# Hybrid RWKV-7 and short-convolution block on one NeuronCore: the usual instruction order, with forms, operand requests, norm and gating as deferred steps

## The chip, the cores and the metric

The kernel runs on one core of one Trainium2 chip. The metric is device time in microseconds; the kernel before took 1043.12 us, the median of three runs (1041.12 to 1046.09). Engines are named as in the profile: PE (TensorE), DVE (VectorE), ACT (ScalarE), POOL (GpSimd), SP (SyncE, which here only issues transfers).

## The reference, cut to what matters

All of it is fp32, with one layer, 512 frames plus 16 meta frames, a model width of 2048 and 8320 projected columns.

```python
hn = _rmsnorm(h_res, norm_in_g[l])
P = hn @ w_in[l]                       # [528, 2048] @ [2048, 8320]
...                                    # r, k, v, g_r, low-rank w and a, token shift
y = _rwkv7_recurrence(rh, decay, kh, vh, kk, kk * ah)    # state per head, frame by frame
yn = (y - mean) * rsqrt(var + LNX_EPS)  # per head
y_a = (yn * lnx_g + lnx_b + bonus) * silu(g_r)
y_b = Bg * causal_conv3(Cg * hc) * silu(g_c)
h_res = h_res + concat([y_a, y_b]) @ w_out[l]
out = _rmsnorm(h_res, norm_f_g)[:, 16:]
```

## The kernel before, in words

**Products.** A product in fp32 is made of three in fp32r: every operand is split into a rounded part and the rest ("low"), and high by high, high by low and low by high are summed in PSUM. Raw weights arrive 512 KB at a time (`request`, L216, on SP's queue). For each quarter of 128x512 `split_w` (L221) makes the high part with an ACT cast (L224) and the low part with a subtraction (L225) on DVE or POOL, as `engines` and the table `ON_POOL` say (L51, L228). The operand tiles for it are six ("hl"). The numbers behind a name in the programs' rows tell buffers of one name apart.

**In-projection.** Its columns go tile by tile. Most are single tiles (L440). The last twelve tiles, of the convolution branch, go as six pairs (`PAIRS`, `pair`, L475): seven products of half matrices (M1, P5, Q6, M3, M7, M2, P4), each of two quarters with twelve matmuls, in place of eight. Their weights are sums of raw tiles (L252, on POOL or DVE), their left operands "forms", sums of x that are brought back from memory and split (`form`, `third_form`, L544/L545). Pair results are added up on DVE as products end (L523, L526, L533), scaled by the norm's factor (`scaled`, L630), and convolved and gated (L667, L668, L716 to L720, L731, L739). After the last pair's M7 `restore` (L612) writes a part of x back (L620, L621).

**Recurrence.** Frames go in chunks of 64. Each chunk's inverse matrices are made ahead for two pairs of heads at a time (`invert`, L1159; on PE L1183, L1197, L1199; copies to SBUF on ACT, L1190). Then `recur` (L1280) runs nine chunks while the pairs' products go on. A chunk's steps on PE are L1297 (needs the state `st`), L1314, and L1352/L1356 (`zs`, `zy`); between them ACT copies results (`pn`, L1305, L1319, L1320) and DVE makes the next state (L1365, L1366). A chunk's operands are `ca` and `cb`, loaded from memory (L1263, on SP). `norm` (L1373) follows at once: sums and centring on DVE (L1382, L1383), squares on ACT (L1388), a reduction on DVE (L1389), the power -0.5 on POOL (L1390, L136), scaling and a transpose on DVE (L1394, L1395), four stores on SP (L1399).

**Order.** PE's order is written by hand: chunk steps and matmuls of pairs are interleaved by `fill` with fixed nanoseconds (`FW`), so each chunk step stands between given products. The orders of ACT, DVE, POOL and SP come from the framework's scheduler, here with `schedule_with_timeline_sim=True` (L1883); every engine takes its instructions strictly in that order. `advance` (L242) prepares weights to eight quarters ahead of the one in use, and requests raw tiles for up to three more where their buffer's last reader has been issued (`free`). `later(ns, fn)` runs a step when PE's written order has come that many nanoseconds further; `ahead()` raises a step's priority.

**Output.** `split_mix` splits the mixed branches, and the out-projection runs in two halves of seven products for four column groups (L1598), its weights loaded and split like the others (L1567), followed by the final norm.

## Time and profile before

| what | value |
|---|---|
| median of 3 runs (lowest, highest) | 1043.12 us (1041.12, 1046.09) |
| the profiled execution's own time | 1044.57 us |
| its span | 1042.8 us |
| its mean granted PE clock | 0.982 |
| busy: PE, DVE, ACT, POOL | 995.9, 758.1, 440.3, 377.4 us |

The span covers the instructions of the profiled execution; its own time has 1.77 us more around it. PE's busy share in the profile's forty slices is 9 tenths nearly everywhere but around the middle of the second half. Four stretches matter below: the single tiles with the preparation of the recurrence (25 to 599 us), the last inversion (599 to 625 us), the six pairs with the recurrence (625 to 850 us), and the start of the out-projection (850 to 925 us).

### The profile page before, as it was taken

Reading aid. Unit: us, or ns where it says so; the run is one execution under the profiler, and the core shown is the slowest. Engines: PE = TensorE matmul, PEld = TensorE weight load, DVE = VectorE, ACT = ScalarE, POOL = GpSimd, SP = SyncE. Lnnn points to the kernel's source line nnn. Section 1 sums busy time; section 2 is a strip of 40 time slices with the busy share of each in tenths; the row PEclk is TensorE's granted clock in tenths of the full one; section 3 lists DMA queues with packets and bytes.
Section 4 is the critical chain, followed back from the end, with each engine's and each line's share of the span. In section 5 each row is a group of like instructions: output and inputs, shape, how many; then the busy total and the mean of one; then the engine's idle time right before and its main releaser. Section 6 shows DMA issues by size and latency. Waiting matters only on the chain. (4 is left out here: it accounts for less than half of the span.)

```text
span 1042.8 us, 24382 instructions
## 1 busy us (share of the span) xinstructions
PE 995.9 (96%) x9867; PEld 927.9 (89%) x9867; DVE 758.1 (73%) x1323; ACT 440.3 (42%) x823; POOL 377.4 (36%) x384
## 2 busy tenths in 40 slices
PE   9999998999999999999999979989879898999996
...
GB/s 312 162 107 154 153 202 170 138 155 150 197 177 156 142 179 132 209 153 143 126 135 169 168 223 278 187 230 174 223 180 99 231 297 230 182 268 193 165 121 162
DMA packets 223216, 188.60 MB, mean 181 GB/s; under 512 B 158720, under 2 KB 187136, under 8 KB 222592
## 3 DMA queue, kind: packets, MB, share of 16 engines
...
q14 instruction: 35, 0.29, 0.1%
...
## 5 line engine op out<-in xcount | busy, mean ns | idle before, releaser
L224 ACT CAST w<-wr 128x512 fp32r<-128x512 f32 x288 | 175.1, 618 | 277.8 <-PE ps_k L440 45.4
L225 POOL TENSOR_TENSOR w<-wr,w 128x512 fp32r<-128x512 f32 x151 | 219.5, 1465 | 181.2 <-ACT w L224 151.2
L225 DVE TENSOR_TENSOR w<-wr,w 128x512 fp32r<-128x512 f32 x137 | 102.8, 753 | 46.6 <-ACT w L224 46.3
L440 PE MATMUL ps_k<-xh,w 128*128 128x272 f32 (+1 forms) x512 | 97.7, 288 | 0.0
L440 PE MATMUL ps_v<-xh,w 128*128 128x256 f32 (+1 forms) x512 | 95.2, 284 | 0.0
L440 PE MATMUL ps_r<-xh,w 128*128 128x258 f32 (+1 forms) x512 | 94.4, 281 | 0.0
L440 PE MATMUL ps_g<-xh,w 128*128 128x256 f32 (+1 forms) x512 | 92.2, 281 | 0.0
L440 PEld LDWEIGHTS ps_k<-xh,w 128*128 128x128 f32 x512 | 82.1, 193 | 0.4
L440 PEld LDWEIGHTS ps_v<-xh,w 128*128 128x128 f32 x512 | 79.9, 188 | 0.3
L440 PEld LDWEIGHTS ps_r<-xh,w 128*128 128x128 f32 x512 | 79.7, 188 | 0.1
L440 PEld LDWEIGHTS ps_g<-xh,w 128*128 128x128 f32 x512 | 78.9, 188 | 0.5 <-DVE gt L1007 0.2
L440 PE MATMUL ps_k<-xl,w 128*128 128x272 f32 (+1 forms) x256 | 73.9, 289 | 0.0
L440 PE MATMUL ps_v<-xl,w 128*128 128x272 f32 (+1 forms) x256 | 72.4, 283 | 0.0
L440 PE MATMUL ps_g<-xl,w 128*128 128x258 f32 (+1 forms) x256 | 72.1, 282 | 0.0
L440 PE MATMUL ps_r<-xl,w 128*128 128x258 f32 (+1 forms) x256 | 72.0, 281 | 0.0
L1553 POOL DMA_DIRECT2D x<-in_w_out_dram x16 | 14.3, 891 | 124.9 <-DVE o L1567 122.0
L440 PE MATMUL ps_h<-xh,w 128*128 128x258 f32 (+1 forms) x320 | 58.7, 283 | 0.0
L440 PE MATMUL ps_C<-xh,w 128*128 128x258 f32 (+1 forms) x320 | 57.7, 281 | 0.0
L252 POOL TENSOR_TENSOR wr<-wr,wr 128x512 f32<-128x512 f32 x24 | 35.2, 1473 | 61.2 <-DVE w L225 27.6
L440 PE MATMUL ps_B<-xh,w 128*128 128x512 f32 x160 | 52.6, 394 | 0.0
L440 PE MATMUL ps_gc<-xh,w 128*128 128x512 f32 x160 | 50.5, 392 | 0.0
L440 PEld LDWEIGHTS ps_h<-xh,w 128*128 128x128 f32 x320 | 50.0, 190 | 0.2
...
## 6 DMA issues: line engine op xcount, KB each, us to landing
...
```

What stands on the lines that cost most here:

```text
L224: state["cast"] = nc.scalar.copy(hi, rq).ins
L225: low[n] = eng.tensor_tensor(out=lo, in0=rq, in1=hi.bitcast(F32), op=ALU.subtract).ins
L252: sum_eng.tensor_tensor(out=x, in0=x, in1=held[extra][:, o : o + 512], op=ALU.add)
L440: nc.tensor.matmul(ps[r], ww[:, w], xx[:, kt, a:b], start=(kt == 0 and n == 0), stop=(kt == KT - 1 and n == 2))
L1553: nc.gpsimd.dma_start(chain[g], rows_of(half, k, col, g), accum_op=ALU.add)
```

## The change

The framework's scheduler is called without its timeline simulation, so ACT, DVE, POOL and SP get the order that it gives by default, by priority and by the order in which the code issues steps. PE's rows are the same ones in the same order. With it:

- `advance` prepares operands six quarters ahead of the one in use instead of eight (`LEAD`), requests raw tiles for five more, and adds raw tiles up to two quarters before their split.
- `ON_POOL`: the lows of M7 and one of the two of P4 go from POOL to DVE; in the first pair those of M3 too. That is eight on POOL per pair before, five after, and three in the first pair.
- Forms: loads and splits are spaced by new numbers (`form`, `split`, `seven`, `six`); four of the eight form lows go to POOL, and so do the lows of the third part, which is now loaded in two pieces.
- `norm`'s squares, reduction with power, scaling with transpose, and stores are four steps at 2500, 4500, 9000 and 10500 ns instead of one step with stores at 7000.
- The gate of the last single tile of the convolution branch waits until after the first pair's P5 copy.
- `ca` and `cb` (apart from the first) are issued on ACT's queue instead of SP's, and at other places of the chunk.
- In the output stage the first group's raw tile is loaded once more (512 KB), lows of the first eight mixed tiles go to POOL, and the explicit waits of `behind_low` are gone.

```diff
@@ -43,14 +43,15 @@
-    tr=3200, lev=3000, cp=4200, out=1500, begin=19500, p=2700, u=2700, s=4700, last=3700, mix=2600, form=1000, split=6000, early=60000, apart=48000,
+    tr=3200, lev=3000, cp=4200, out=1500, begin=19500, p=2700, u=2700, s=4700, last=3700, mix=2600, form=200, split=1500, seven=6000, six=9000, early=60000, apart=48000,
 )
-AHEAD, WEIGHTS, FORMS = 6000, 3000, 2000
+AHEAD, WEIGHTS, LEAD = 6000, 3000, 6
+NORM = (2500, 4500, 9000, 10500)
 ON_POOL = {
-    "M1": ((), ()), "P5": ((), ()), "Q6": ((), ()), "M3": ((0, 1), ()), "M7": ((0, 1), (0, 1)), "M2": ((0, 1), ()),
-    "P4": ((0, 1), (0, 1)),
+    "M1": ((), ()), "P5": ((), ()), "Q6": ((), ()), "M3": ((0, 1), ()), "M7": ((), (0, 1)), "M2": ((0, 1), ()),
+    "P4": ((1,), (0, 1)),
 }
@@ -214,7 +216,10 @@
     def request(n):
-        held[n] = chain[n - N_IN] if n >= N_IN else raw_tile(place_of[n], f"wr{n}")
+        if n == N_IN:
+            order.append(order.pop(0))
+            place_of[n] = order[-1]
+        held[n] = chain[n - N_IN] if n > N_IN else raw_tile(place_of[n], f"wr{n}")
         state["dma"] = nc.sync.dma_start(held[n], raws[n]).ins
@@ -230,7 +235,7 @@
             return nc.gpsimd if (n % 2 or late) and 22 < n < S_IN else nc.vector, None
-        low_on, sum_on = ON_POOL[kind[2][0]]
+        low_on, sum_on = ON_POOL["P5" if kind[2][0] == "M3" and n < FIRST_PAIR + 14 else kind[2][0]]
         return (nc.gpsimd if kind[2][1] in low_on else nc.vector), (nc.gpsimd if kind[2][1] in sum_on else nc.vector)
@@ -239,19 +244,28 @@
-    def advance(upto, more=0):
+    def add_up(n):
+        kind, r, o, extra = slots[n]
+        if extra is not None and n not in summed:
+            summed.add(n)
+            x = held[r][:, o : o + 512]
+            engines(n)[1].tensor_tensor(out=x, in0=x, in1=held[extra][:, o : o + 512], op=ALU.add)
+
+    summed = set()
+
+    def advance(upto, more=0, ahead=0):
         end = len(slots) if chain else S_IN
...
             kind, r, o, extra = slots[n]
-            low_eng, sum_eng = engines(n)
             with tc.high_priority(offset=WEIGHTS):
-                x = held[r][:, o : o + 512]
-                if extra is not None:
-                    sum_eng.tensor_tensor(out=x, in0=x, in1=held[extra][:, o : o + 512], op=ALU.add)
-                split_w(n, x, low_eng)
+                add_up(n)
+                split_w(n, held[r][:, o : o + 512], engines(n)[0])
             state["slot"] = n + 1
+            for m in range(n + 1, min(n + 1 + ahead, end)):
+                if slots[m][3] is not None and last_raw(m) < state["raw"]:
+                    add_up(m)
         for n in range(state["slot"], min(upto + more, end)):
@@ -503,19 +521,22 @@
                 state["used"] += 1
-                advance(state["used"] + 8, 3)
+                advance(state["used"] + LEAD, 9 - LEAD + 2, 2)
...
             with ahead():
-                nc.scalar.copy(t[:, 0:n], ps[:, 0:n])
+                state["sum"] = nc.scalar.copy(t[:, 0:n], ps[:, 0:n]).ins
...
         copy(v, B, n_t)
+        if "mixed" in state:
+            with tc.issue_after(state["sum"]):
+                state.pop("mixed")()
         yield from product("Q6", A, n_t)
@@ -574,40 +594,49 @@
         dims, fp = [P, 3, W2], shared_pools[1]
-        t = fp.tile(dims, F32, tag=f"f{KA // 2 + k}", name=f"sum{k}") if k < KA // 2 else temporary(k, f"sum{k}", dims)
-        f = fp.tile([P, 2, 3, LF], F32R, tag=f"f{k}", name=f"forms{k}")[:, :, :, 8 : 8 + W2]
+        if k < 3:
+            t = fp.tile(dims, F32, tag=f"f{4 + k}", name=f"sum{k}")
+        elif k == 3:
+            rest.append(fp.tile([P, 2] + dims[1:], F32, tag="f7", name="sum3"))
+            t = rest[0][:, 0]
+        elif k == 6:
+            t = rest[0][:, 1]
+        else:
+            t = temporary(0 if k == 4 else 1, f"sum{k}", dims)
         nc.sync.dma_start(t, fsum[:, k, 0:3])
         def part():
-            with tc.issue_after(state["ts"]) if k >= 4 else nullcontext():
-                apart(f[:, 0], f[:, 1], t, nc.vector)
-
-        later(FW["split"], part)
-        sfr.append(f)
-
-    thirds = []
+            f = fp.tile([P, 2, 3, LF], F32R, tag=f"f{k}", name=f"forms{k}")[:, :, :, 8 : 8 + W2]
+            sfr[k] = f
+            with tc.issue_after(state["tm"]) if k > 5 else nullcontext():
+                apart(f[:, 0], f[:, 1], t, nc.vector if k in (0, 1, 3, 5) else nc.gpsimd)
+
+        later(FW["split"] if k < 6 else FW["six"] + 500 * k, part)
+
+    rest, thirds = [], {}
     def load_third(j):
-        a, b = 3 * j, min(3 * j + 3, KA)
-        t = temporary(min(j, 1), f"third{j}", [P, 3, W2])[:, 0 : b - a]
+        a, b = ((0, 3), (3, KA))[j]
+        t = (
+            cqt([P, 5 * W2], F32, tag="g", name="third1").rearrange("p (k w) -> p k w", k=5)
+            if j else temporary(0, "third0", [P, 3, W2])
+        )
         nc.sync.dma_start(t, fsum[:, a:b, 3])
-        thirds.append((slice(a, b), t))
+        thirds[j] = (slice(a, b), t)
...
         shared_pools.append(shared.enter_context(tc.tile_pool(name="fp", bufs=1, reuse_waits="tile")))
-        for k in range(KA):
+        for k in range(7):
             later(FW["form"] * k, lambda k=k: form(k))
+        later(FW["form"] * 7, lambda: load_third(1))
+        later(FW["seven"], lambda: form(7))
+        later(FW["seven"] + 500, lambda: load_third(0))
+
+    def third_form():
         for j in range(2):
-            later(FW["form"] * KA, lambda j=j: load_third(j))
-
-    def third_form():
-        assert len(thirds) == 2
-        for j in range(3):
             k, t = thirds[j]
-            apart(xh[:, k, T0X:XW], xl[:, k, T0X:XW], t, nc.vector)
-            if j == 1:
-                load_third(2)
+            apart(xh[:, k, T0X:XW], xl[:, k, T0X:XW], t, nc.gpsimd)
@@ -734,11 +764,18 @@
                 scaled(REAL, ps, g, META)
-            gate(g, f"c{i}")
-            o = direct.get(8 + i, cv)
-            nc.vector.scalar_tensor_tensor(out=o, in0=cv, scalar=0.5, in1=g, op0=ALU.mult, op1=ALU.mult)
-            if o is cv:
-                later(9000, lambda: nc.sync.dma_start(mixd[8 + i], cv))
+
+            def mixed():
+                gate(g, f"c{i}")
+                o = direct.get(8 + i, cv)
+                nc.vector.scalar_tensor_tensor(out=o, in0=cv, scalar=0.5, in1=g, op0=ALU.mult, op1=ALU.mult)
+                if o is cv:
+                    later(9000, lambda: nc.sync.dma_start(mixd[8 + i], cv))
+
+            if i == 3:
+                state["mixed"] = mixed
+            else:
+                mixed()
         ready.add((what, i))
@@ -1258,9 +1295,9 @@
-    def load_ops(t, c, pairs, part):
+    def load_ops(t, c, pairs, part, queue=nc.scalar):
         a, b = pairs
-        nc.sync.dma_start(
+        queue.dma_start(
             t[:, a:b],
@@ -1304,6 +1343,9 @@
             if c and not last:
+                if c == 1:
+                    second[2] = new_second(ch, 2)
+                    load_ops(second[2], 2, (0, 4), 1)
                 load_ops(second[c + 1], c + 1, (4, 8), 1)
@@ -1312,12 +1354,12 @@
                         nc.tensor.matmul(z[e][hs, 1, k], t[m, O_X : O_X + CH], pn[m, e, k], start=True, stop=True)
-            if not last:
-                first[c + 1] = load_first(ch, c + 1)
             u = pn
...
                 nc.scalar.copy(u[:, 1], z[1][:, 1])
+            if not last:
+                first[c + 1] = load_first(ch, c + 1)
             fill(FW["u"])
@@ -1354,9 +1396,6 @@
                         nc.tensor.matmul(d[ho, j], t[hs, o : o + CH], x[hs], start=(a == 0), stop=(a == b - 1))
-            if c + 2 < NCH:
-                second[c + 2] = new_second(ch, c + 2)
-                load_ops(second[c + 2], c + 2, (0, 4), 1)
             if not last:
@@ -1378,21 +1417,33 @@
-        for z, j in zip(zs, (slice(0, NPAIR - 1), slice(NPAIR - 1, NPAIR))):
+        for z, j in zip(zs[::-1], (slice(NPAIR - 1, NPAIR), slice(0, NPAIR - 1))):
             nc.vector.tensor_reduce(out=nv[:, 0, j], in_=z, op=ALU.add, axis=AX.X)
...
         yq = yt.rearrange("p (j s) -> p j s", s=CH)
-        with tc.issue_after(state["cast"]):
+
+        def scale():
+            nc.vector.tensor_reduce(out=nv[:, 1], in_=yq, op=ALU.add, axis=AX.X)
+            nc.gpsimd.tensor_scalar(
+                out=nv[:, 2], in0=nv[:, 1], scalar1=1.0 / CH, scalar2=LNX_EPS, op0=ALU.mult, op1=ALU.add
+            )
+            rsqrt(nv[:, 3], nv[:, 2])
+
+        def turn():
+            nc.vector.tensor_tensor(out=yc, in0=yc, in1=spread(3), op=ALU.mult)
+            nc.vector.transpose(yt, yc.rearrange("p j s -> p (j s)"))
+
+        def square():
             nc.scalar.activation(yq, yc, AF.Square)
-        nc.vector.tensor_reduce(out=nv[:, 1], in_=yq, op=ALU.add, axis=AX.X)
-        nc.gpsimd.tensor_scalar(
-            out=nv[:, 2], in0=nv[:, 1], scalar1=1.0 / CH, scalar2=LNX_EPS, op0=ALU.mult, op1=ALU.add
-        )
-        rsqrt(nv[:, 3], nv[:, 2])
-        nc.vector.tensor_tensor(out=yc, in0=yc, in1=spread(3), op=ALU.mult)
-        nc.vector.transpose(yt, yc.rearrange("p j s -> p (j s)"))
+            if c + 2 < NCH:
+                second[c + 2] = new_second(ch, c + 2)
+                load_ops(second[c + 2], c + 2, (0, 4), 1)
+
+        later(NORM[0], square)
+        later(NORM[1], scale)
+        later(NORM[2], turn)
@@ -1405,7 +1456,7 @@
-        later(7000, put)
+        later(NORM[3], put)
@@ -1677,6 +1726,8 @@
             if half == 0:
+                if g == 0:
+                    at(-1, begin_chain, 0, g)
                 if g == 3:
@@ -1880,7 +1927,7 @@
     args.append(nc.dram_tensor("out_0_dram", (SEQ, DM), F32, kind="ExternalOutput").ap())
-    with tile.TileContext(nc, schedule_with_timeline_sim=True) as tc:
+    with tile.TileContext(nc) as tc:
         hymba_kernel(tc, *args)
```

Three places show how the rows move. The first is DVE at the end of the fifth pair's products, around the state of the sixth chunk (`st_10363` before, `st_10346` after); `yc` and `yt` are the norm's tiles, `gc` and `cv` the gate and the convolution's result, `w` an operand tile, `wr` raw weights. Before:

```order
L630 TENSOR_TENSOR gc_10191<-sums_B_gc_9653,rs 128x256
L252 TENSOR_TENSOR wr_9817<-wr_9817,wr_9947 128x512
L225 TENSOR_TENSOR w_10101<-wr_9817,w_10101 128x512
L1394 TENSOR_TENSOR yc_10062<-yc_10062,nv_10061 128x512
L1395 STREAM_TRANSPOSE yt_10063<-yc_10062 128x512
L630 TENSOR_TENSOR gc_10191<-ps_B_gc_A,rs 128x256
L225 TENSOR_TENSOR w_10117<-wr_9817,w_10117 128x512
L668 SCALAR_TENSOR_TENSOR gc_10191<-th_c_10194,gc_10191 128x512
L739 SCALAR_TENSOR_TENSOR cv_9646<-cv_9646,gc_10191 128x512
L1365 TENSOR_TENSOR st_10363<-zs_10279,st_10058 128x512
```

After:

```order
L1428 TENSOR_REDUCE nv_10044<-yt_10046 128x8
L659 TENSOR_TENSOR gc_10178<-ps_B_gc_A,rs 128x256
L230 TENSOR_TENSOR w_10173<-wr_9801,w_10173 128x512
L1435 TENSOR_TENSOR yc_10045<-yc_10045,nv_10044 128x512
L697 SCALAR_TENSOR_TENSOR gc_10178<-th_c_10181,gc_10178 128x512
L1436 STREAM_TRANSPOSE yt_10046<-yc_10045 128x512
L771 SCALAR_TENSOR_TENSOR cv_9629<-cv_9629,gc_10178 128x512
L230 TENSOR_TENSOR w_10255<-wr_9877,w_10255 128x512
L1404 TENSOR_TENSOR st_10346<-zs_10264,st_10041 128x512
```

The gate's second part from PSUM (L630 before, L659 after) stood behind the norm's scaling and transpose, and now stands ahead of both; the gate's products stay ahead of the state.

The second is DVE in the last pair (`xl` is the part of x that `restore` writes back). Before:

```order
L523 TENSOR_TENSOR sums_B_gc_10734<-ps_B_gc_B,sums_B_gc_10734 128x256
L630 TENSOR_TENSOR b_11048<-sums_B_gc_10734,rs 128x256
L1394 TENSOR_TENSOR yc_10922<-yc_10922,nv_10921 128x512
L621 SCALAR_TENSOR_TENSOR xl<-again_11024,pvt,xh 128x258 x2
L1395 STREAM_TRANSPOSE yt_10923<-yc_10922 128x512
L621 SCALAR_TENSOR_TENSOR xl<-again_11030,pvt,xh 128x258
L526 TENSOR_TENSOR sums_B_gc_10734<-sums_B_gc_10734,ps_B_gc_A 128x256
L621 SCALAR_TENSOR_TENSOR xl<-again_11030,pvt,xh 128x258
L621 SCALAR_TENSOR_TENSOR xl<-again_11036,pvt,xh 128x258 x2
```

After:

```order
L544 TENSOR_TENSOR sums_B_gc_10718<-ps_B_gc_B,sums_B_gc_10718 128x256
L659 TENSOR_TENSOR b_11034<-sums_B_gc_10718,rs 128x256
L1428 TENSOR_REDUCE nv_10906<-yt_10908 128x8
L547 TENSOR_TENSOR sums_B_gc_10718<-sums_B_gc_10718,ps_B_gc_A 128x256
L659 TENSOR_TENSOR b_11034<-sums_B_gc_10718,rs 128x256
L650 SCALAR_TENSOR_TENSOR xl<-again_11010,pvt,xh 128x258 x2
L1435 TENSOR_TENSOR yc_10907<-yc_10907,nv_10906 128x512
L1436 STREAM_TRANSPOSE yt_10908<-yc_10907 128x512
L554 TENSOR_TENSOR sums_B_gc_10718<-ps_B_gc_C,sums_B_gc_10718 128x256
```

The sum that empties M7's PSUM bank, into which PE's P4 goes (L526, now L547), has moved ahead of the norm's scaling and of all rows that write x back.

The third is ACT in the last inversion (`ts` is the copy that PE's L1197 reads). Before:

```order
L224 CAST w_7766<-wr_7761 128x512
L544 CAST forms_7854<-sum_7853 128x3x258
L544 CAST forms_7866<-sum_7865 128x3x258
L224 CAST w_7803<-wr_7801 128x512
L544 CAST forms_7878<-sum_7877 128x3x258
L544 CAST forms_7890<-sum_7889 128x3x258
L1190 COPY ts_0_7927<-t_0_7893 128x512
L1190 COPY ts_1_7928<-t_1_7894 128x512
```

After:

```order
L229 CAST w_7763<-wr_7761 128x512
L229 CAST w_7766<-wr_7761 128x512
L1227 COPY ts_0_7948<-t_0_7914 128x512
L1227 COPY ts_1_7949<-t_1_7915 128x512
L229 CAST w_7803<-wr_7801 128x512
L229 CAST w_7806<-wr_7801 128x512
L564 CAST forms_7882<-sum_7853 128x3x258
```

The two copies (L1190, now L1227) stood behind four casts of forms, and now stand ahead of all of them.

56 lines of the change are left out of this document (28 added, 28 removed).

## The prediction

> **What bounds the kernel now.** I read the table by stretch first, then PE's timeline for its stops, then the chain of waits and the other engines' timelines at those stops. Columns of the first: stretch, length, busy us (instructions) of PE, weight loads, DVE, ACT and POOL, granted PE clock, DMA share, GB/s.
>
> ```profile
> 25.00:599.00 574.00, 568.73 (x5288) 548.64 (x5286) 386.13 (x771) 223.97 (x409) 201.19 (x233) 0.99 0.63 158
> 599.00:625.00 26.00, 20.06 (x289) 16.18 (x283) 19.85 (x30) 13.50 (x22) 4.32 (x3) 0.93 0.69 219
> 625.00:850.00 225.00, 206.22 (x3394) 197.47 (x3383) 169.01 (x235) 88.34 (x182) 144.44 (x105) 0.95 0.70 208
> 850.00:925.00 75.00, 68.79 (x293) 55.43 (x292) 68.37 (x90) 35.24 (x59) 12.99 (x11) 0.98 0.78 215
> ```
>
> PE is the bound: in the single tiles it idles 574 - 568.73 = 5.3 us. In the pairs it idles 225 - 206.22 = 18.8 us, and four stops make up most of that; two more stand in the last inversion. In brackets is the idle time and what ended it.
>
> ```profile
> 601.67 1.13 PE L1183 MATMUL t<-xn,gt 64*64 64x64 f32 x32 [2.46 <-DVE xn L1174]
> 609.43 0.33 PE L1197 MATMUL z<-xT,ts 64*64 64x64 f32 x4 [2.11 <-ACT ts L1190]
> 698.55 0.71 PE L1297 MATMUL rz<-st,ca 64*64 64x64 f32 x6 [3.01 <-issue]
> 737.25 0.71 PE L1297 MATMUL rz<-st,ca 64*64 64x64 f32 x6 [3.83 <-DVE st L1366]
> 769.96 0.37 PE L1352 MATMUL zs<-pn,cb 64*64 64x64 f32 x2 [5.08 <-ACT pn L1319]
> 820.87 0.55 PE L500 MATMUL ps_B_gc_A<-xh,w 128*128 128x256 f32 x1 [2.92 <-DVE sums_B_gc L526]
> ```
>
> The four sum to 3.01 + 3.83 + 5.08 + 2.92 = 14.84 us, so small stops hold 18.8 - 14.8 = 4.0. Behind each of the four PE runs some 6 us at a lower clock:
>
> ```profile
> 698.50:704.00 5.50, 5.34 (x84) 5.20 (x85) 2.66 (x6) 3.11 (x7) 3.49 (x4) 0.69 0.54 142
> 737.20:743.00 5.80, 5.65 (x87) 5.45 (x88) 2.98 (x6) 3.52 (x9) 3.79 (x4) 0.71 0.40 128
> 769.90:776.00 6.10, 6.04 (x167) 5.92 (x168) 4.95 (x7) 1.60 (x5) 5.11 (x4) 0.53 0.82 188
> 820.80:826.30 5.50, 5.43 (x25) 5.46 (x26) 4.66 (x8) 0.62 (x1) 3.97 (x3) 0.50 0.66 146
> ```
>
> That loses 5.5 x 0.31 + 5.8 x 0.29 + 6.1 x 0.47 + 5.5 x 0.50 = 1.7 + 1.7 + 2.9 + 2.75 = 9.0 us. Stops and clock together are 23.8 us. The chain behind the first (start, us, what):
>
> ```profile
> 670.80 8.14 POOL w L225 x6
> 678.97 8.37 DMA wr<-in_w_in_dram
> 687.44 1.80 DVE wr L252
> ...
> 695.21 1.57 DVE cv L739
> 696.78 0.61 DVE st L1365
> 697.41 1.03 DVE st L1366
> ```
>
> POOL's lows are the last readers of a raw tile; only then SP requests the next, which lands 8.37 us later; its sum and the gate stand ahead of the state on DVE. SP's waits and the waits for landing and power in this stretch (us in total, times, longest):
>
> ```profile
> SPq L218 <- POOL w L225: 70.6, 21, 8.6
> SPq L1399 <- DVE yt L1395: 51.8, 5, 16.9
> POOL wr L252 <- DMA wr<-in_w_in_dram: 27.0, 4, 9.0
> DVE yc L1394 <- POOL nv L136: 11.9, 7, 3.2
> ```
>
> **The change part by part.** *Third stop (769.96).* DVE, then ACT:
>
> ```profile
> 765.67 1.75 DVE L1394 TENSOR_TENSOR yc<-yc,nv 128x512 f32<-128x512 f32 x1 [1.54 <-POOL nv L136]
> 767.45 0.71 DVE L1395 STREAM_TRANSPOSE yt<-yc 128x512 f32<-128x512 f32 x1
> 768.08 0.39 DVE L630 TENSOR_TENSOR gc<-ps_B_gc_A,rs 128x256 f32<-128x256 f32 x1
> ...
> 768.50 0.63 ACT L667 ACTIVATE th_c<-gc 128x512 f32<-128x512 f32 x1 [4.25 <-DVE gc L630]
> ...
> 769.55 0.36 ACT L1319 COPY pn<-rz 128x256 f32<-128x256 f32 x1
> ```
>
> ACT's copy for PE stands behind the gate's activation, that behind DVE's L630, that behind the norm's scaling and transpose, and those wait for POOL's power. The order shown puts L630 ahead of both: it could start at 765.67 - 1.54 = 764.1, 4.0 us earlier. So 4.0 of 5.08 go, and 4/5 of the 2.9 of clock: -6.3. Late next is DVE's reduction, now directly ahead, which waits for ACT's squares.
>
> *Fourth stop (820.87).* The last matmul of M7, then DVE:
>
> ```profile
> 814.84 0.28 PE L500 MATMUL ps_B_gc_A<-xh,w 128*128 128x256 f32 x1
> ...
> 813.82 1.77 DVE L1394 TENSOR_TENSOR yc<-yc,nv 128x512 f32<-128x512 f32 x1 [0.60 <-POOL nv L136]
> 815.52 2.96 DVE L621 SCALAR_TENSOR_TENSOR xl<-again,pvt,xh 128x258 fp32r<-128x258 f32 x2
> ...
> 820.32 0.41 DVE L526 TENSOR_TENSOR sums_B_gc<-sums_B_gc,ps_B_gc_A 128x256 f32<-128x256 f32 x1
> ```
>
> All that stands between 813.82 and L526 now comes behind it. M7 had ended at 815.1, and PE idled from 820.87 - 2.92 = 817.95, so DVE has time for that sum: the stop goes whole, -2.92 - 2.75 = -5.7.
>
> *First and second stop.* Here DVE's rows ahead of the state stay (gate; convolution L716 to L720). What changes is the loop: fewer POOL lows ahead of SP's request. POOL and DVE prices of a low in this stretch, mean ns behind the comma:
>
> ```profile
> L225 POOL TENSOR_TENSOR w<-wr,w 128x512 fp32r<-128x512 f32 x61 | 87.7, 1463 | 13.1 <-ACT w L224 12.3 <-DMA mix<-yd 0.8
> ...
> L225 DVE TENSOR_TENSOR w<-wr,w 128x512 fp32r<-128x512 f32 x34 | 27.8, 817 | 10.0 <-ACT w L224 10.0
> ```
>
> Three lows less per pair are 3 x 1.46 = 4.4 us, more than either stop, but SP's stores of the norm still stand ahead of some requests. Bounds are nothing and all, (3.01 + 1.7) + (3.83 + 1.7) = 10.2; I take half, -5.1. The four stops: -6.3 - 5.7 - 5.1 = -17.1.
>
> *Small stops.* Between 0 and -4.0; the same loop, -1.0.
>
> *Last inversion.* ACT:
>
> ```profile
> 603.48 1.65 ACT L544 CAST forms<-sum 128x774 fp32r<-128x774 f32 x2 [8.81 <-DMA sum<-fsum]
> ...
> 607.08 1.81 ACT L544 CAST forms<-sum 128x774 fp32r<-128x774 f32 x2 [1.44 <-DMA sum<-fsum]
> ...
> 608.80 1.07 ACT L1190 COPY ts<-t 128x512 f32<-128x512 f32 x2
> ```
>
> The two copies stood behind casts that wait for a transfer; now they stand ahead of them. The stop of 2.11 goes, with half of the stretch's lost clock, 26 x 0.07 / 2 = 0.9: -3.0. The 2.46 (a transpose on DVE) stays.
>
> *What the change adds.* About twenty lows on DVE (three in each of five later pairs, five in the first): 20 x 0.817 = 16.3 us, while POOL sheds 20 x 1.463 = 29.3. A low newly stands directly ahead of the state in two of the chunks: 2 x 0.82 = +1.6 on the path. Form and third lows on POOL would be 1463 x 774/512 = 2.2 us each, an estimate; POOL is busy 4.32 us of 26 there, so nothing, or 3 x 1.46 x 774/512 = 6.6 if the pairs wait for three. `ca` and `cb` on ACT's queue: ACT is busy 88 of 225 us, so nothing; a saving is not to be had where SP's waits above are for POOL and DVE. The Trainium skill, "DMA: Bandwidth & Descriptors", section "Issuing engines are not separate DMA queues", speaks against a gain as well: transfers issued by ScalarE, SyncE or GpSimd end up on the same engines, and several issuers save only issue time. By that the term is nothing, as it is by the rows.
>
> *The usual order in the first 600 us.* DVE's, ACT's and POOL's rows stand otherwise there too. To gain are at most the 5.3 us of idle; to lose, a stop per preparation. With DVE busy 386 of 574 us and ACT and POOL under 40% there is slack; I take one stop like the 2.46: +2.5.
>
> *Output stage.* One more transfer of 512 KB, while DVE is busy 68 of 75 us and PE idle 6.2. Between -2.9, the size of the fourth stop, for the dropped waits and +8.4, a landing; nothing taken, since DVE's work is the same.
>
> **Sum.** -17.1 - 1.0 - 3.0 + 1.6 + 2.5 = -17.0 on the profiled execution's own 1044.57 (span 1042.8 and 1.77 around it): 1027.6. That execution stands 1.45 above the median 1043.12, so about 1026.
>
> A rule would make it less: the Trainium skill, "TensorE: Matmul & The Clock Gate", Part 1, says the clock drops to half after an idle window of about 3.4 us, so only the second and third stop would cost clock. By it the stop terms are 6.3 + 2.8 + 2.9 + 1.5 = 13.5, an estimate, and the sum 1030. The rows differ: 0.69 behind 3.01 us idle and 0.50 behind 2.92. So of the forecast's chance below only 0.05 goes by that rule.
>
> **Rivals.** *All stops go* (0.13): the loop gets time enough and DVE keeps up. 23.8 + 4.0 + 3.0 = 30.8 off 1043.1: 1012. For it speaks that the loop is one mechanism; against it that DVE's gate and convolution rows still precede the state.
>
> *DVE becomes the bound* (0.13): 169 + 16.3 = 185 us in a stretch of some 207 is 90%. Half of the stop terms return: 1026 + 8.6 = 1035.
>
> *Requests come too late* (0.10): with six quarters for eight, a tile's last reader is issued two quarters later, hence the request. Two quarters are one product:
>
> ```profile
> 692.50 3.04 PE L500 MATMUL ps_C_h_B<-forms,w 128*128 128x258 f32 x24
> ```
>
> Six pairs x 3.04 = 18.2 us would eat the gain: 1044, no change. Against it: what released tiles in the trace is POOL's queue, not the written lead.
>
> *The usual order opens stops in the single tiles* (0.14), the case on the other side. There are eight preparations and four inversions from 25 to 599 us, now covered. A stop as in the pairs costs 23.8 / 4 = 6.0 with its clock. The gains are 21.1, less 1.6: 19.5; slower by over 0.5% (5.2 us) takes 24.7, so it decides from five such stops, at 1043.1 - 19.5 + 30 = 1054. For it: DVE is already at 67% there and its order is strict. Against it: the slack just named.
>
> **How the numbers follow.** My forecast, 1026, has 0.50; its own range is 1014 to 1036 (the unknown halves both ways, the 6.6 of POOL). About 0.5% is what a measurement here tells from no change. Faster: 0.50 + 0.13 + 0.13 = 0.76; same 0.10; slower 0.14. The range 1010 to 1044 leaves out the slower case and the far end of the best one.
>
> **What would show it.** Right: no PE stop over 2 us at the fifth pair's chunk and at the last pair's P4, the clock of 625 to 850 us at 0.97 or more, the L1197 stop gone, PE idle below 10 us there. Wrong: PE stops for operand tiles in the single tiles, DVE over 90% in the pairs with waits on lows, or requests on SP still 8 us behind POOL.

## The result, and the profile after

The changed kernel takes 1035.34 us, the median of five runs (1032.14 to 1037.22); the kernel before, beside it, takes 1042.35. The ratio is 0.9925, with a 95% interval from 0.9899 to 0.9952. The direction was right and the time lies in the range, but the gain is 7.0 us where 17 were forecast. The profiled execution took 1036.30 us, with a span of 1034.5 and a mean granted clock of 0.980 (0.982 before).

The table by stretch, changed kernel (columns as in the prediction):

```profile
25.00:599.00 574.00, 570.58 (x5335) 549.33 (x5333) 390.96 (x782) 224.44 (x413) 201.75 (x235) 1.00 0.62 162
599.00:625.00 26.00, 24.88 (x298) 20.64 (x298) 17.58 (x24) 11.75 (x20) 15.48 (x10) 1.00 0.45 153
625.00:850.00 225.00, 206.60 (x3347) 196.96 (x3346) 185.36 (x255) 88.88 (x180) 127.84 (x92) 0.95 0.72 210
850.00:925.00 75.00, 68.04 (x271) 54.10 (x270) 67.29 (x87) 36.05 (x60) 13.81 (x14) 0.91 0.81 236
```

PE is fuller in the single tiles (idle 3.4 us, was 5.3), much fuller in the stretch of the last inversion (1.1, was 5.9), and as idle as before in the pairs (18.4, was 18.8), with the same clock of 0.95. These are stretches of time, and the changed kernel is up to 14 us ahead in them, so their ends hold other work than before. From matmul to matmul of the table further down, PE idles 4.7 us in the first pair (633.1 to 649.7; none before) and 13.7 in the recurrence (649.7 to 859.3; 18.8 before). In the pairs DVE took over 16.4 us and POOL shed 16.6. PE's timeline, the stops that matter, with the idle time before them and what ended it:

```profile
630.76 1.66 PE L518 MATMUL ps_C_h_B<-forms,w 128*128 128x258 f32 x6 [3.11 <-DVE w L230]
643.95 0.29 PE L1336 MATMUL rz<-cb,ca 64*64 64x64 f32 x4 [1.58 <-DMA cb<-opd]
693.13 0.33 PE L1336 MATMUL rz<-st,ca 64*64 64x64 f32 x4 [2.51 <-issue]
709.85 0.58 PE L518 MATMUL ps_C_h_A<-xl,w 128*128 128x258 f32 x1 [3.20 <-issue]
783.99 0.37 PE L518 MATMUL ps_C_h_C<-xh,w 128*128 128x256 f32 x1 [3.46 <-issue]
863.39 1.30 PE L1647 MATMUL M<-w,m 128*128 128x512 f32 x2 [3.25 <-DVE gc L668]
880.59 3.65 PE L1647 MATMUL P<-o,S 128*128 128x512 f32 x7 [3.22 <-ACT o L1617]
```

Of the four stops of before, the first is still there (2.51 us, was 3.01) and the other three are gone. New ones have come in the first pair (630.76) and at two places where the profile shows no operand that PE waited for (709.85 and 783.99). In the output stage the same two waits, for DVE's `gc` and ACT's `o`, were there before and have grown (2.23 and 2.12 us before). At the third stop's place the rows of DVE moved as forecast: the gate's part from PSUM, which ACT's gate and so its copy for PE wait for, now stands 3 us ahead of the norm's scaling, which waits for POOL's power:

```profile
756.32 0.41 DVE L659 TENSOR_TENSOR gc<-ps_B_gc_A,rs 128x256 f32<-128x256 f32 x1
...
759.32 1.76 DVE L1435 TENSOR_TENSOR yc<-yc,nv 128x512 f32<-128x512 f32 x1 [1.82 <-POOL nv L137]
```

The clock behind the new stop in the first pair and behind the two at "issue", in the table by stretch:

```profile
630.00:634.00 4.00, 3.21 (x13) 2.91 (x14) 3.88 (x7) 2.25 (x5) 1.42 (x2) 0.55 0.54 94
709.80:715.50 5.70, 5.65 (x26) 5.65 (x27) 0.94 (x2) 1.25 (x2) 0.00 (x0) 0.50 0.64 159
783.90:790.00 6.10, 6.01 (x55) 5.88 (x57) 5.33 (x13) 2.50 (x4) 2.75 (x2) 0.72 0.04 7
```

PE issues the same 9867 matmuls in the same order in every program of this study, so the starts of one and the same matmul can be compared. The table gives how much earlier (minus) or later it starts than in the kernel before, in each one's profiled execution, in us. The places, with the time before: the last inversion (601.8), the last matmuls ahead of the first pair's forms (633.1), the end of the first chunk's first step (649.7), two places in the recurrence (718.4, 777.6), the last single tile (859.3), two in the output stage (902.5, 1015.5). The upper part of the program is the same in nearly all the variants, and still their figures at 601.8 spread over 3 us; differences below that are not read.

```
kernel      601.8  633.1  649.7  718.4  777.6  859.3  902.5 1015.5   ratio [95%]
changed      -6.9  -11.0   -2.8    0.2  -14.3  -10.8   -5.1   -8.1   0.9925 [0.9899, 0.9952]
b_usual      -8.9  -14.3    0.2   -1.7   -7.5   -8.6   -7.9  -10.3   0.9934 [0.9912, 0.9956]
a_sim         1.3   -1.8   -1.9    1.9    4.8    6.6   19.6   17.7   1.0190 [1.0129, 1.0252]
a_norm       -9.8  -13.9   -5.3   -3.9   -7.1   -3.8    0.6   -1.4   1.0004 [0.9977, 1.0031]
a_sp         -8.9  -13.0   -1.7    3.1   -2.3   -3.9    1.9   -0.6   0.9974 [0.9951, 0.9997]
a_formq      -8.0  -13.2   -7.7   -7.5  -21.2  -17.4  -10.9  -13.8   0.9872 [0.9822, 0.9922]
a_dve        -9.5  -14.8   -9.8  -12.0  -22.0  -20.7  -14.2  -17.2   0.9859 [0.9808, 0.9910]
a_out        -8.3  -12.5   -1.8   -1.4  -15.2  -11.7   -9.2  -11.3   0.9881 [0.9822, 0.9941]
a_pool       -9.0  -13.1   -3.8   -1.8  -15.1  -11.6   -4.6   -7.6   0.9916 [0.9886, 0.9945]
a_lead8      -8.8  -12.9   -2.6   -0.7  -14.8  -12.3   -6.1   -9.1   0.9907 [0.9872, 0.9942]
a_more3     -10.1  -14.3   -5.1   -2.1   -7.6   -4.3   -0.5   -1.9   0.9996 [0.9973, 1.0020]
a_noca      -10.2  -14.3   -4.3   -5.9  -17.6  -20.2  -14.5  -17.6   0.9856 [0.9816, 0.9896]
a_noops      -8.8  -13.0   -4.4   -6.6  -10.6  -12.8   -6.7   -9.3   0.9922 [0.9887, 0.9957]
best1        -8.5  -13.8   -4.8   -4.5  -18.1  -15.3  -13.0  -15.1   0.9840 [0.9800, 0.9880]
best2        -8.1  -13.5   -7.4   -4.2  -18.7  -15.4  -12.6  -14.7   0.9848 [0.9815, 0.9881]
```

Read the first row: 11.0 us are won ahead of the first pair, 8.3 of them are lost in it, 8.1 are won in the recurrence, and the output stage loses 5.7 and gets 3.0 back.

**Where the 11 us come from.** DVE's transpose for the last inversion, before and after:

```profile
600.91 0.71 DVE L1174 STREAM_TRANSPOSE xn<-xT 128x512 f32<-128x512 f32 x1 [5.05 <-DMA xT<-sx]
```

```profile
590.28 0.71 DVE L1211 STREAM_TRANSPOSE xn<-xT 128x512 f32<-128x512 f32 x1 [1.06 <-DMA xT<-sx]
```

SP's transfer for it, before and after:

```profile
596.50 0.60 SPq L1123 DMA_DIRECT2D xT<-sx  x1
```

```profile
585.37 0.60 SPq L1160 DMA_DIRECT2D xT<-sx  x1
```

The inverse's round trip through memory (`sx`, `xT`) is issued 11 us earlier, so PE no longer waits for the transpose. The stop of 2.46 us that the forecast left standing is gone, with the slow clock of the stretch (0.93 before, 1.00 now).

**Where 8 us go.** SP at the first pair, the longest of its waits there (us in total, times, longest), then POOL and DVE, changed kernel. The last two lines are SP's first loads of `cb`, before and after:

```profile
594.90 0.33 SPq L223 DMA_DIRECT2D wr<-in_w_in_dram  x1
612.64 0.32 SPq L606 DMA_DIRECT2D sum<-fsum  x1
```

```profile
SPq L606 <- DVE forms L565: 11.8, 1, 11.8
```

```profile
623.57 3.44 POOL L252 TENSOR_TENSOR wr<-wr,wr 128x512 f32<-128x512 f32 x2
626.98 3.18 POOL L565 TENSOR_TENSOR xl<-third,xh 128x1290 fp32r<-128x1290 f32 x1
```

```profile
620.10 1.29 DVE L230 TENSOR_TENSOR w<-wr,w 128x512 fp32r<-128x512 f32 x2 [6.29 <-ACT w L229]
...
624.29 1.58 DVE L230 TENSOR_TENSOR w<-wr,w 128x512 fp32r<-128x512 f32 x1
...
628.82 1.88 DVE L230 TENSOR_TENSOR w<-wr,w 128x512 fp32r<-128x512 f32 x1
...
631.96 0.69 DVE L230 TENSOR_TENSOR w<-wr,w 128x512 fp32r<-128x512 f32 x1
```

```profile
633.84 3.27 SPq L1263 DMA_DIRECT2D cb<-opd  x4
```

```profile
635.20 1.14 SPq L1300 DMA_DIRECT2D cb<-opd  x2
```

Form 7's load (L606) goes into a buffer that an earlier form's low on DVE must free; it waits 11.8 us for that in one piece, and the next raw weights stand behind it until 613.49. So their splitting starts late: DVE is idle for 6.29 us until 620.10. The copies of the last inverse (`xT`, L1285) stand between the rows for these weights on DVE, and the loads of `cb`, which read that inverse back from memory, come after them. PE is 11 us ahead, but the first load of `cb` is issued 1.4 us later than before. DVE's rows are also slower: a low takes 1.58 us beside POOL's sum of raw tiles and another 1.88 beside POOL's third, for 0.69 at 631.96, when POOL is idle. PE waits 3.11 us for such a low, then 1.58 for the first chunk's `cb`, and between the two runs slower: the clock is 0.50 from 630.4 to 637.2 us, which at 6.4 us of busy PE loses about 3.2, and the three make up the 8 us. Part of that is only that PE is early and `cb` isn't, as a_sim suggests: there the same lows are on POOL, though in another order, PE is 1.8 us ahead, and it loses nothing here.

### The profile page after: what moved, and what is told of

Read it like the earlier page. It is cut to its first block, busy times and chain, and to the rows that moved or that the text cites. A ratio compares the mean times of both kernels' runs of the same rounds, so it can differ in the third digit from the quotient of the medians.

```text
span 1034.5 us, 24353 instructions
## 1 busy us (share of the span) xinstructions
PE 995.3 (96%) x9867; PEld 926.4 (90%) x9867; DVE 771.0 (75%) x1328; ACT 439.0 (42%) x822; POOL 372.4 (36%) x378
## 3 DMA queue, kind: packets, MB, share of 16 engines
q8 instruction: 77, 1.26, 0.5%
## 4 chain that ended last, share of the span: by engine, by line
PE 71%; DVE 15%; DMA 6%; issue 4%; POOL 2%; ACT 1%; SPq 0%; DVEq 0%; ACTq 0%; POOLq 0%
PE ps_g L456 9%; PE ps_v L456 9%; PE ps_r L456 8%; PE ps_k L456 8%; PE M L1647 5%; PE ps_h L456 4%; PE ps_C L456 4%; PE P L1647 3%; PE ps_B L456 3%; PE ps_gc L456 3%; DVE w L230 2%; PE ps_C_h_A L518 2%; DMA wr<-in_w_in_dram 2%; PE Q L1647 2%; DMA x<-in_w_out_dram 2%
## 5 line engine op out<-in xcount | busy, mean ns | idle before, releaser
L230 POOL TENSOR_TENSOR w<-wr,w 128x512 fp32r<-128x512 f32 x131 | 189.8, 1453 | 238.2 <-ACT w L229 223.5
L230 DVE TENSOR_TENSOR w<-wr,w 128x512 fp32r<-128x512 f32 x159 | 130.6, 832 | 84.1 <-ACT w L229 83.9
L456 PE MATMUL ps_k<-xh,w 128*128 128x272 f32 (+1 forms) x512 | 95.4, 284 | 0.0
L456 PEld LDWEIGHTS ps_k<-xh,w 128*128 128x128 f32 x512 | 80.0, 188 | 0.4
L252 POOL TENSOR_TENSOR wr<-wr,wr 128x512 f32<-128x512 f32 x24 | 38.2, 1600 | 51.4 <-DVE w L230 17.6
```

Of the source, the lines that this page charges most:

```text
L230: low[n] = eng.tensor_tensor(out=lo, in0=rq, in1=hi.bitcast(F32), op=ALU.subtract).ins
L252: engines(n)[1].tensor_tensor(out=x, in0=x, in1=held[extra][:, o : o + 512], op=ALU.add)
L456: nc.tensor.matmul(ps[r], ww[:, w], xx[:, kt, a:b], start=(kt == 0 and n == 0), stop=(kt == KT - 1 and n == 2))
```

## The experiments

Each edit is to the changed kernel unless the text says otherwise.

**b_usual and a_sim: the order and the steps apart.** b_usual is the kernel before with the usual order; a_sim is the changed kernel with the simulated one.

```diff
-    with tile.TileContext(nc, schedule_with_timeline_sim=True) as tc:
+    with tile.TileContext(nc) as tc:
```

> The kernel before, with the scheduler's usual order and nothing else of the change. Theory A: the order carries the gain of the single tiles (PE reached the end of the last inversion's copies 11.0 us earlier in the changed kernel, of it 6.9 by its first transposes), so PE stands 5 to 9 us earlier at 600 us here too, while the pairs, for whose steps the deferrals were written, lose: stops of 6 to 20 us more in the pairs, 1042 to 1055 in all. Theory B: the deferred steps carry the gain: PE at 600 us within 2 us of before, 1043 or more.

> The changed kernel's code, ordered by the timeline simulation as before. Theory A (order carries the single tiles' gain): PE at 600 us within 2 us of before, and 1037 to 1043 in all. Theory B (deferred steps carry the gain): 1030 to 1036.

b_usual: 0.9934 [0.9912, 0.9956]; a_sim: 1.019 [1.0129, 1.0252]. PE's stops of b_usual, then of a_sim:

```profile
629.95 2.30 PE L500 MATMUL ps_C_h_A<-forms,w 128*128 128x258 f32 x9 [4.22 <-ACT sums_C_h L513]
644.59 0.70 PE L1297 MATMUL rz<-cb,ca 64*64 64x64 f32 x16 [5.85 <-DMA cb<-opd]
...
755.02 0.37 PE L1297 MATMUL rz<-st,ca 64*64 64x64 f32 x2 [4.56 <-DVE yc L1383]
813.35 0.36 PE L500 MATMUL ps_B_gc_A<-xh,w 128*128 128x256 f32 x1 [3.07 <-DVE sums_B_gc L526]
```

```profile
602.93 1.14 PE L1220 MATMUL t<-xn,gt 64*64 64x64 f32 x32 [4.84 <-DVE xn L1211]
...
890.42 2.05 PE L1647 MATMUL M<-w,m 128*128 128x512 f32 x4 [12.82 <-DVE gc L668]
```

The first theory of b_usual had half: PE is 8.9 us ahead at 601.8, but the median is 1036.78 us where it said 1042 or more. a_sim, at 1062.16, is slower than both of its theories. The usual order alone has the whole net gain, and the gain ahead of the first pair is the order's: it stands in b_usual and not in a_sim, where the transpose is late again. The other parts of the change are worth nothing on top in sum (some gain and some lose, as the next runs show), and under the simulated order they cost 1.9%. b_usual loses even more at the first pair (14.5 us), by waits for a copy on ACT and for `cb`.

**a_norm: the norm in one piece again.**

```diff
-        later(NORM[0], square)
-        later(NORM[1], scale)
-        later(NORM[2], turn)
+        square()
+        scale()
+        turn()
...
-        later(NORM[3], put)
+        later(7000, put)
```

> The changed kernel with the norm's steps all at once, its stores at 7000, as before. Theory H: the deferral frees the gate and the state: without it the stop at the fifth pair's chunk comes back (3 to 5 us with 2 to 3 of clock), 1040 to 1044. Rival: the usual order alone keeps the norm's scaling away from the gate: within 2.5 us of the changed kernel, 1033 to 1038.

1.0004 [0.9977, 1.0031], so the deferral is worth 8 us, with the loads of `cb` that stand in `square` and move with it. PE has a stop in the chunk of the third one of before again, though one step of the chunk earlier (L1356, not L1394), and the fourth at the same matmul as before:

```profile
759.03 1.39 PE L1356 MATMUL rz<-pn,ca 64*64 64x64 f32 x32 [6.50 <-ACT pn L1344]
...
818.18 0.36 PE L518 MATMUL ps_B_gc_A<-xh,w 128*128 128x256 f32 x1 [3.89 <-DVE sums_B_gc L547]
```

**a_sp: `ca` and `cb` on SP's queue again.**

```diff
-    def load_ops(t, c, pairs, part, queue=nc.scalar):
+    def load_ops(t, c, pairs, part, queue=nc.sync):
-    def load_first(ch, c, queue=nc.scalar):
+    def load_first(ch, c, queue=nc.sync):
```

> The changed kernel with ca and cb issued on SP as before. Theory C: two PE stops in the recurrence of the changed kernel (709.85, 3.20 us; 783.99, 3.46 us; ended by nothing that the profile shows) are PE out of code, since its 16 KB code transfer starts 3.6 and 4.6 us late behind data transfers, and the second issuing queue lets 2.3 MB start at once. Then both stops fall below 1 us, about 8 to 11 us with the slow clock behind them: 1024 to 1030. Rival: they are operands that come late by the shorter lead; the queue changes nothing there: 1033 to 1038.

0.9974 [0.9951, 0.9997]: the move to ACT's queue is worth some 5 us, though the two intervals just touch. Theory C fell: the two stops at "issue" stay (3.23 and 2.21 us), and 1042.38 us lies outside both ranges. The matmul of the third stop of before waits again, though the norm is deferred:

```profile
767.69 0.37 PE L1394 MATMUL zs<-pn,cb 64*64 64x64 f32 x2 [3.38 <-ACT pn L1359]
```

Two of SP's waits in the recurrence of a_sp (total us, times, longest):

```profile
SPq L1300 <- PE rz L1356: 6.2, 2, 5.8
...
SPq L1300 <- PE zy L1398: 5.4, 2, 4.6
```

A load of `ca` or `cb` waits for PE's last reader of its buffer, and on SP every raw weight behind it waits too. On ACT's queue it holds up ACT instead (12.3 us in two waits for `cb` in the changed kernel), which is busy 88.9 of 225 us and seems to have the time.

**a_pool, a_lead8, a_more3: where lows stand, and how far ahead.** a_pool undoes the table of lows. Requests reach eleven quarters ahead before (8 + 3) as in the changed kernel (6 + 5); a_lead8 goes back to 8 + 3, and a_more3 makes it 6 + 3, nine in all.

```diff
-    "M1": ..., "M7": ((), (0, 1)), "M2": ((0, 1), ()), "P4": ((1,), (0, 1)),
+    "M1": ..., "M7": ((0, 1), (0, 1)), "M2": ((0, 1), ()), "P4": ((0, 1), (0, 1)),
...
-        low_on, sum_on = ON_POOL["P5" if kind[2][0] == "M3" and n < FIRST_PAIR + 14 else kind[2][0]]
+        low_on, sum_on = ON_POOL[kind[2][0]]
```

```diff
-AHEAD, WEIGHTS, LEAD = 6000, 3000, 6
+AHEAD, WEIGHTS, LEAD = 6000, 3000, 8
```

```diff
-            advance(state["used"] + LEAD, 9 - LEAD + 2, 2)
+            advance(state["used"] + LEAD, 3, 2)
```

> The changed kernel with the lows split between POOL and DVE as before (eight of a pair on POOL). Theory: POOL's lows hold the raw tiles, as the prediction had it for the first and second stop, so requests come later again: 1038 to 1043. Rival: DVE is the one short of time in the pairs (185 us of 225 in the changed kernel), and gains by it: 1028 to 1034.

> The changed kernel with operands prepared eight quarters ahead and three more requests, as before. Rival of the prediction (requests too late with six): 1030 to 1034, PE earlier in every pair. If the lead only moves ACT's casts behind other work: within 2.5 us of the changed kernel, 1033 to 1038; longer if casts that wait for a free operand tile block ACT's copies, 1039 to 1044.

> The changed kernel with raw tiles requested for three more quarters instead of five. Theory C (PE's code transfer starts late behind data): fewer raw tiles are under way when the chunk's small matmuls use up code, so the two code stops (matmul 7095 and 8498 of PE's order; 3.20 and 3.46 us) shrink below 2 us; but weights land later: 1031 to 1040. Rival: the stops stay at 3 us or more.

a_pool 0.9916 and a_lead8 0.9907 can't be told from the changed kernel's 0.9925; a_more3 is at 0.9996 [0.9973, 1.002]. The row of 625 to 850 us of a_pool:

```profile
625.00:850.00 225.00, 207.19 (x3342) 197.56 (x3343) 169.31 (x235) 87.37 (x180) 155.51 (x111) 0.95 0.72 210
```

Its stop at the place of the first one of before:

```profile
692.28 0.46 PE L1336 MATMUL rz<-st,ca 64*64 64x64 f32 x4 [1.86 <-issue]
```

DVE is back at 169 us and POOL up at 155, and the time is the same, between the two ranges that were expected: neither POOL's lows nor DVE's busy share sets it. How far requests reach does matter: the five only make up for the shorter lead, and three cost 7 us. The two stops at "issue" hardly shrink in a_more3 (3.01 and 2.27 us; the expectation was below 2), and the fourth stop of before is back, at the same matmul, with the norm deferred:

```profile
817.67 0.53 PE L518 MATMUL ps_B_gc_A<-xh,w 128*128 128x256 f32 x1 [4.10 <-DVE sums_B_gc L547]
```

**a_formq and a_dve: the first pair.** a_formq takes the two loads that wait out of SP's queue; a_dve puts all form and third lows on DVE.

```diff
-        nc.sync.dma_start(t, fsum[:, k, 0:3])
+        (nc.gpsimd if k == 7 else nc.sync).dma_start(t, fsum[:, k, 0:3])
...
-        nc.sync.dma_start(t, fsum[:, a:b, 3])
+        (nc.sync if j else nc.gpsimd).dma_start(t, fsum[:, a:b, 3])
```

```diff
-                apart(f[:, 0], f[:, 1], t, nc.vector if k in (0, 1, 3, 5) else nc.gpsimd)
+                apart(f[:, 0], f[:, 1], t, nc.vector)
...
-            apart(xh[:, k, T0X:XW], xl[:, k, T0X:XW], t, nc.gpsimd)
+            apart(xh[:, k, T0X:XW], xl[:, k, T0X:XW], t, nc.vector)
```

> The changed kernel with the loads of form 7 and of the third part's first piece issued on POOL's queue, so that SP's raw requests do not stand behind them (594.90, then 613.49 in the changed kernel). Theory D: the operand stop in the first pair (630.76, 3.11 us) comes from these late requests: it goes, PE is 3 to 6 us earlier behind the first pair (646.9 in the changed kernel at the matmul where before had 649.7), 1029 to 1033 in all. Rival E: the first chunk's operands set the pace there (stores of the inverse until 632.6, then 2.4 MB of ca and cb that land at 643.9): the stop for cb grows by what the other loses, PE within 1.5 us of the changed kernel there, 1034 to 1037.

> The changed kernel with all lows of forms and third part on DVE, as before. Theory F: POOL's long lows slow DVE beside them (sums and lows of 128x512 took 1.34 to 2.25 us on DVE at 621.9 to 630.7, against 0.68 alone): the rows fall below 1 us, the copies of the inverse and so ca and cb come earlier, PE 2 to 5 us earlier behind the first pair, 1030 to 1034. Rival: DVE's 8 us more of work cost as much as they save: within 2 us there, 1034 to 1038.

0.9872 [0.9822, 0.9922] and 0.9859 [0.9808, 0.991]. PE's stop in the first pair, a_formq and then a_dve (3.11 in the changed kernel):

```profile
627.53 2.16 PE L518 MATMUL ps_C_h_B<-forms,w 128*128 128x258 f32 x10 [2.25 <-DVE w L230]
```

```profile
627.33 3.01 PE L518 MATMUL ps_C_h_A<-forms,w 128*128 128x258 f32 x15 [1.18 <-DVE w L230]
```

At 649.7 they are 4.9 and 7.0 us further ahead than the changed kernel, 2.2 and 3.8 of it at 633.1 already (near the spread of the table). In a_formq the stop that was to go has only shrunk, and the time (1030.31) is as expected. a_dve gives DVE more work and is faster. The rows did not all fall below 1 us, as its theory had it (a low of DVE still takes 1.73 us at 617.65, beside POOL's sum); what moved is the inverse and so `cb`, whose first load is issued at 627.57 in a_dve and 628.91 in a_formq, for 635.20.

**a_out: the output tile loaded once.**

```diff
-        if n == N_IN:
-            order.append(order.pop(0))
-            place_of[n] = order[-1]
-        held[n] = chain[n - N_IN] if n > N_IN else raw_tile(place_of[n], f"wr{n}")
+        held[n] = chain[n - N_IN] if n >= N_IN else raw_tile(place_of[n], f"wr{n}")
...
-                if g == 0:
-                    at(-1, begin_chain, 0, g)
```

> The changed kernel without the second load of the out-projection's first raw tile. Theory G: the two stops of 3.2 us at 863 and 880 with their slow clock (PE lost 5.7 us on before between 848 and 897) come of 512 KB more on busy queues: the second falls below 1.5 us, 3 to 5 us less, 1030 to 1032. Rival: they come of the dropped waits or of DVE's order: unchanged within 1.5 us, 1034 to 1037.

0.9881 [0.9822, 0.9941]. PE's stop at 880.59 is gone, while the one at 863 stays, for ACT's `w` now (4.34 us). From the last single tile to the last place of the table a_out loses 0.4 us for the changed kernel's 2.7; best1 and best2, which have the same edit, lose 0.2 and 0.7, and all variants with the second load and the usual order lose 2.4 to 4.0. The interval of a_out reaches over the changed kernel's, so the times alone (some 4 us) don't show it; the trace gives 2 to 3 us.

**a_noca and a_noops: the two stops at "issue".** The DMA view of the changed kernel from 706.7 to 709.9 us, around the stop that ends at 709.85 (packets, MB, share of the 16 DMA engines):

```profile
q1 hardware_dynamic: 194, 0.68, 71.8%
q10 hardware_dynamic: 154, 0.22, 21.7%
q8 instruction: 1, 0.02, 2.1%
```

One 16 KB packet of code (q8) ran from 707.49 to 708.57, and PE went on 1.28 us after its end; for the second stop it ran from 781.75 to 782.75, and PE went on 1.25 us after. Before, the same two matmuls (the 7095th to 7098th and the 8498th to 8501st) had waited 0.67 and 0.54 us, 1.26 and 1.43 us after such a packet. Between the two places PE has 1403 matmuls and the queue eleven packets, 128 matmuls for each, which fits code of PE. a_noca leaves out the loads of `ca` behind the first chunk's, a_noops those of `cb` too.

```diff
-                first[c + 1] = load_first(ch, c + 1)
+                first[c + 1] = first[c]
```

```diff
...
-                    second[2] = new_second(ch, 2)
-                    load_ops(second[2], 2, (0, 4), 1)
-                load_ops(second[c + 1], c + 1, (4, 8), 1)
+                    second[2] = second[0]
...
-                second[c + 2] = new_second(ch, c + 2)
-                load_ops(second[c + 2], c + 2, (0, 4), 1)
+                second[c + 2] = second[c]
```

> The changed kernel without the loads of ca behind the first (all chunks compute with the first chunk's ca: 768 KB x 8 less on the queues). Theory C: code no longer waits at 709.85 and 783.99; both stops below 1 us, 1022 to 1029. Rival (late operands of the weights, or an unseen wait for something else): both stops stay at 2 us or more, 1032 or more.

> The changed kernel without any load of recurrence operands after the first two chunks': all eight chunks compute with the first chunk's ca and, by turns, the first and the second chunk's cb (so the mixture that comes out of the recurrence is another). Instructions on PE, DVE and POOL stay as they are. Theory C (code comes late because data stand ahead of it in the DMA engines): PE's two pauses ended by issue, 3.20 us at 709.85 and 3.46 us at 783.99 in the changed kernel, fall under 0.8 us each and the clock behind them stays at 0.9 or more; with their clock that is 8 to 10 us, so 1017 to 1027. Rival (the sequencer asks late for its code, whatever the data do): both pauses stay at 2 us or more at the same matmuls, and the time only drops as far as raw weights land sooner, 1027 to 1033.

(There are nine chunks, not eight as the expectation of a_noops has it.) a_noca: 0.9856 [0.9816, 0.9896], with the second stop gone and the first smaller:

```profile
706.50 0.28 PE L518 MATMUL ps_C_h_A<-xl,w 128*128 128x258 f32 x1 [1.79 <-issue]
```

a_noops: 0.9922 [0.9887, 0.9957], both gone. The table by stretch of a_noops, then its PE stops in the recurrence:

```profile
625.00:850.00 225.00, 207.14 (x3342) 196.64 (x3341) 186.24 (x254) 88.02 (x179) 124.98 (x91) 0.95 0.48 134
...
709.80:715.50 5.70, 5.70 (x126) 5.37 (x129) 5.24 (x7) 2.66 (x6) 3.86 (x4) 1.00 0.09 15
```

```profile
692.06 0.33 PE L1336 MATMUL rz<-st,ca 64*64 64x64 f32 x4 [2.63 <-DVE nv L1419]
...
728.87 0.33 PE L1336 MATMUL rz<-st,ca 64*64 64x64 f32 x4 [2.04 <-DVE nv L1419]
...
759.56 0.37 PE L1392 MATMUL zs<-pn,cb 64*64 64x64 f32 x2 [3.38 <-ACT pn L1357]
```

Each theory of a_noops had half. That code comes late because data stand ahead of it is borne out: with the DMA share down from 0.72 to 0.48 both stops are gone, and the clock behind the first place is 1.00. (Less thorough thinning, by the queue in a_sp or by fewer requests in a_more3, had left both over 2 us.) But the time stayed where it was, outside both ranges: the first wait shown is the changed kernel's 2.51, but the other two, for DVE and for ACT, have come up in place of the two stops, where the changed kernel has none over 2 us. One reading is that DVE and ACT had caught up while PE stood for code. But a_noca, which takes away less, is 7 us faster and wins 15.9 us from 649.7 to 859.3, where a_noops wins 8.4 and the changed kernel 8.1. PE idles only 2.5 us less there in a_noca, so most of the difference is clock (0.98 and 0.95 from 625 to 850), behind waits of the same kind. From 754 to 765 us, a_noca (behind a wait of 2.22 us for ACT) and a_noops (behind the 3.38):

```profile
754.00:765.00 11.00, 10.08 (x275) 9.81 (x276) 9.12 (x12) 6.66 (x16) 7.97 (x6) 1.00 0.64 165
```

```profile
754.00:765.00 11.00, 7.62 (x182) 7.30 (x182) 9.67 (x13) 3.61 (x8) 8.20 (x5) 0.69 0.17 27
```

What makes the waits for DVE and ACT shorter in a_noca is not shown, so whether the two stops at "issue" cost the changed kernel their 10 us or nothing stays open.

**best1 and best2: together.** best1 is a_dve, a_formq and a_out in one; best2 leaves a_formq out.

> The changed kernel with three parts undone or moved: all lows of forms and third part on DVE, form 7 and the third part's first piece issued on POOL's queue, no second load of the out-projection's first tile. If the three costs (6 to 7, 5, 4 us against the changed kernel) are separate they sum: 1019 to 1023. If the first two are one wall, the start of the first pair, only one of them counts: 1024 to 1028.

> The changed kernel with all lows of forms and thirds on DVE and without the second load of the first output tile, but with the two loads of forms on SP's queue as in the changed kernel. If the cures of the first pair are one and the same slack, the load of forms is already out of the way when DVE does the lows in time, and the ratio is 0.983 to 0.986, as with the two loads on POOL's queue (0.984). If the loads on POOL's queue are worth something of their own, the ratio is 0.987 to 0.991 and PE waits over 2 us for an operand tile (w) in the first pair.

best1: 0.984 [0.98, 0.988], 1027.25 us; best2: 0.9848 [0.9815, 0.9881], 1029.02. Both beat the kernel before and the changed one; neither can be told from a_dve alone (0.9859). The gains don't add: at 649.7 best1 keeps 4.8 us where a_dve alone kept 9.8. In its timeline PE has no stop over 1 us inside the first pair, but a longer one behind it, for the first chunk's `cb`:

```profile
637.67 0.46 PE L1333 MATMUL rz<-cb,ca 64*64 64x64 f32 x16 [3.87 <-DMA cb<-opd]
```

best2 is as fast as best1, so the queue of the two loads is worth nothing measurable on top of lows that end in time.

## Why the prediction was right or wrong

- **The step that failed** is the sum over the recurrence: forecast -16.5 (-17.1, -1.0, +1.6), measured -8.1 (from -2.8 at 649.7 to -10.8 at 859.3). It took each stop off with its clock as if nothing were late behind it. The runs showed two stops at "issue" in their place, with their clock some 10 us (3.20 + 3.46 - 0.67 - 0.54, and 5.7 x 0.50 + 6.1 x 0.28). Behind these, a_noops shows waits for DVE and ACT of 2.04 and 3.38 us and wins no more (8.4), while a_noca wins 15.9; which of the two holds for the changed kernel stays open. Of the four signs that the prediction named for being right, two came (the stops of the third and fourth place, and of L1197, are gone) and two did not: the clock stayed at 0.95 and PE idles 18.4 us from 625 to 850.
- **Third and fourth stop** (-6.3 and -5.7): the mechanism holds, but it is not the only one. Both are gone. With the norm in one piece 6.50 us stand in the third one's chunk and 3.89 at the fourth; the 8 us of a_norm stand against the 12.0 of the two terms. The usual order alone leaves 3.07 at the fourth (b_usual). And with the norm deferred the third comes back at 3.38 us in a_sp, and the fourth at 4.10 in a_more3, so the queue of the loads and the reach of the requests hold them off as well.
- **First and second stop** (half, by POOL's lows): the reason was wrong. The first stays at 2.51 us, and a_pool, with POOL's lows back, has no stop over 2 us at either place (1.86 us at 692.28). b_usual has only 1.04 us at the second, so the order took that away.
- **Last inversion** (-3.0, "the 2.46 stays") **and the usual order in the first 600 us** (+2.5): wrong, the second in sign. Together they measured -11.0 by 633.1, for -0.5. I had looked at what the order could delay, and not at the round trip through memory that it issues earlier.
- **Form and third lows on POOL** ("nothing, or 6.6"): nothing was taken, and 8.3 us are lost between 633.1 and 649.7. Not all of it is the lows: with them on DVE, a_dve still loses 5.0 there, best1 9.0, and b_usual, which never had them on POOL, 14.5. By the times, moving them back is worth 6.9 us. POOL had been idle, but DVE, which worked beside it, slowed down; the row of SP that the forms' loads were put into was never costed, nor `cb`, which sets the pace behind. That 11.0 won and 8.3 lost leave -2.8 at 649.7, near the forecast's -0.5, is luck: two errors against each other.
- **`ca` and `cb` on ACT's queue** (nothing): wrong, worth some 5 us by a_sp. The waits that I read on SP were for POOL and DVE; the same view of before has 4.8 us for PE as well (`SPq L1263 <- PE zs L1352: 4.8, 2, 4.6`), and SP's order passes such waits on to what stands behind. The Trainium skill, "DMA: Bandwidth & Descriptors", section "Issuing engines are not separate DMA queues", says that a second issuer saves only issue time; here it seems to have saved the waits that a_sp's rows show on SP, 6.2 and 5.4 us.
- **Output stage** (0): measured +2.7, near the middle of its bounds; without the second load of the raw tile (a_out) it is +0.4.
- **The rivals.** "DVE becomes the bound" named 1035, which is what came, with its 185 us of DVE; but a_pool brings DVE back to 169 without a gain, so the number was met and the cause not shown. "Requests come too late" falls for this kernel: a_lead8 changes nothing. Requests that reach less far do cost 7 us (a_more3), but the change keeps their reach. "The usual order opens stops in the single tiles" falls: PE idles less there.
- **The clock rule** weighed there (the Trainium skill, "TensorE: Matmul & The Clock Gate", Part 1: half clock after an idle window of about 3.4 us) is not met as a threshold: the clock was 0.50 from 692.3 to 699 us of a_pool, behind 1.86 us idle, 0.55 behind 3.11 and 0.50 behind 3.20 in the changed kernel, and 1.00 behind the 2.22 of a_noca.
